# Numbering background convolution work 240 places later in a list-scheduled hybrid decoder layer

## The chip, the cores and the metric

The kernel runs on one core of a Trainium2 chip. The time is the device time of one execution in microseconds (us); less is better. The core's engines each work off a queue of their own: TensorE (PE; its weight loads are listed apart as PEld), VectorE (DVE), ScalarE (ACT), GpSimd (POOL) and SyncE (SP, which here only issues DMAs). An engine starts its instructions in the order of its queue.

## The reference

One layer of a hybrid decoder over a prompt of 2048 tokens and 8 single decode tokens, in fp32, with a model width of 1024:

```python
z = rms_norm(x, norm_mix_g) @ w_in
q, k, v, cu = jnp.split(z, [Q_END, K_END, V_END], axis=-1)
q = rope(rms_norm(q.reshape(B, T, N_HEADS, HEAD_DIM), q_norm_g), pos)
...
attn_o = banded_swa(q, k, v, attn_sinks)
...
a, g = jnp.split(cu, 2, axis=-1)
glu = a * jax.nn.sigmoid(g)
conv_ext = jnp.concatenate([conv_hist.astype(glu.dtype), glu], axis=1)
conv_o = jax.nn.silu(layer_norm(causal_dwconv(conv_ext, conv_w, conv_b), conv_ln_g, conv_ln_b))
h = x + jnp.concatenate([attn_o, conv_o], axis=-1) @ w_out
```

Attention has 8 heads of 64 over 2 key heads, a window of 128 and a sink per head. The convolution branch has 512 channels: a gated linear unit, a causal depthwise convolution of 31 taps, a LayerNorm over the channels, and swish. After it come a gated ConvFFN (2816 columns) and a sigmoid-gated per-layer embedding, which the change does not touch.

## The kernel before, in words

Every product that must be exact to fp32 is split into a high and a low part: `hilo` (line 211) copies the source to a reduced format on ACT and subtracts it on DVE, and `mm3` (line 194) multiplies three times on PE (lines 195 to 197).

**The attention stretch** goes through the prompt in four quarters of 512 tokens. A quarter has 12 slots, written out by hand in `orders` (line 867). An "a" slot is `ag_unit` (line 838): 24 matmuls of 512 columns into a PSUM tile, then a sigmoid on ACT (line 854) or, in every second unit, a product on DVE (line 860) and a store of the gated rows to DRAM. A "q" slot is `qkv_unit` (line 819): 48 matmuls (lines 828 to 833) into the tiles `pq` and `pk`, and a generator `attn_block` (line 588) that is taken forward by one stage in each of the next slots. In its stages the block normalizes and rotates q and k (DVE lines 532 to 578, POOL lines 221, 222, 539 and 576), transposes them on PE (lines 596 and 599) and copies them out split (line 213), multiplies scores (line 621), adds the mask and takes the minimum on DVE (line 627, one instruction per head, followed by a read of its accumulator), takes exponentials on ACT (line 631), reciprocals on DVE (line 636) and scales on ACT (line 639), transposes the probabilities (line 648) and multiplies by v (lines 659 to 662, tile `O`). Between quarters, `norm_x` (line 261) normalizes the next 512 rows and `xn_k` (line 308) transposes them (line 313). The first output-projection units follow in `w_out_unit` (line 776).

All transposes and small products of the kernel, those of the LayerNorm too, use the PSUM tag "T" (`ttile`, line 66), of which there are two buffers. The tiles of one tag get their buffers in program order: on PE the writers of T tiles stand in the order in which the program makes the tiles. The wide products of the stretch use the tag "mm", with four buffers.

**The background work** is the convolution. `conv_piece` (line 388) is a generator for one quarter: for each of four groups of 128 channels it loads 542 gated columns (line 397 or 399), multiplies once (line 408) and then adds 30 taps into the same tile, one `scalar_tensor_tensor` of 128x512 each (line 411), and at the end it runs `layer_norm` (line 427): three adds, a mean by a matmul on PE (`lnm`, line 435), a copy on ACT, subtractions, squares, a sum over channels on PE (`lnv`, line 455), a power on POOL, a transpose that spreads it (`lnb`, line 463), products, swish on ACT and a store from ACT's DMA queue (line 473). `bg(2500)` (line 510) is called after each slot and takes some five taps from the list. Two pieces are on the list in the attention stretch; the other two quarters are convolved in the feed-forward stretch.

**What sets the order.** The program runs once and numbers every instruction with a counter, `tc.cur_priority`. When it has ended, the framework's list scheduler goes through a modelled execution: whenever an engine is free in it, that engine gets, of the instructions whose inputs and buffers are ready, the one with the lowest number. The order so found is the order of each engine's queue on the chip. `bg` keeps the counter in `p0` and puts it back at its end, so the taps of a slot and the foreground of the next slot share the same numbers. Where a tap and foreground instructions are ready together, the lower number goes first; where only a tap is ready, it goes, however high its number. `later` (line 415) adds to the counter for a few instructions; the LayerNorm's PE instructions have 60 more that way.

Of the kernel before, what the change touches and what calls it, by code (L numbers as in the profile page):

```python
# [33 lines left out]
def hybrid_layer_kernel(ctx: ExitStack, tc: tile.TileContext, I, O):  # L34
# [472 lines left out]
    bg_list = []  # L507
    step_ns = [0]

    def bg(ns):  # L510
        p0 = tc.cur_priority
        while bg_list and ns > 0:
            try:
                c = next(bg_list[0])
            except StopIteration:
                bg_list.pop(0)
                continue
            if c == -1:
                break
            ns -= step_ns[0] if c is None else c  # L520
        tc.cur_priority = p0
# [197 lines left out]
    def new_R(nm, where, dt=F32R):  # L719

        return [RP[w].tile([128, 2, RW], dt, tag=f"R{w}", bufs=(16, 12)[w - 1], name=nm) for w in where]
# [157 lines left out]
    for q in range(4):  # L879
        ia = iq = 0  # L880
        L = len(orders[q])
        for si, ch in enumerate(orders[q]):
# [9 lines left out]
            else:  # L892
# [4 lines left out]
                live.append(ent)  # L897
            run_live()
            bg(2500)
            if q < 3:  # L900
                if si == (4, 2, 2)[q]:
# [31 lines left out]
    while live:  # L933
        w_out_unit(0, Rm0, mo, C0, acc)
        mo += 1
        run_live()
        bg(2500)
        slot += 1
# [122 lines left out]
        return range(n * (m - first) // c, n * (m - first + 1) // c) if m >= first else []  # L1061

    step_ns[0] = 1300
    Rm1 = new_R("mixA1", [1] * 8)
    for m in range(mo, KD):
        w_out_unit(0, Rm0, m, C0, acc)
        if m == 4:
            while bg_list:
                bg(1e9)
        elif m < 4:  # L1070
            bg(4000)
        fill_mix(Rm1, 0, 512, 512, ks=spread(m, mo))
        if m > 4:
            dec_step()
# [484 lines left out]
```

## Time and profile before

| | before |
|---|---|
| median of 3 runs (lowest to highest) | 2437.38 us (2435.72 to 2438.55) |
| the profiled execution | 2442.29 us |
| its span, first to last instruction | 2440.5 us |
| mean granted clock of TensorE | 0.987 |

The profile is of one execution. Its groups give, for each line and engine, the number of instructions, their busy time and the mean of one; its windows give the busy time of each engine in a stretch of the span, the clock that the throttle granted to PE as a share of full speed, the DMA engines' share and GB/s. A window's rows name, in this order, the stretch, its length, and then PE, PEld, DVE, ACT and POOL with their counts. The waits name an engine's instruction, what released it, the total, the number of times and the longest. The attention stretch takes about the first 500 us of the span, and its 240 taps (line 411) are 184.7 us of DVE's time between 50 and 500 us:

```profile
L411 DVE SCALAR_TENSOR_TENSOR co<-gi,cvec,co 128x512 f32<-128x512 f32 x240 | 184.7, 787 | 2.4
```

### The profile page before, as it was taken

How to read it: one execution, taken by the hardware profiler on the slowest of the kernel's cores; microseconds unless marked ns; L12 is line 12 of the kernel's file. 1: busy time of each engine (PE TensorE's matmuls, PEld its weight loads, DVE VectorE, ACT ScalarE, POOL GpSimd, SP SyncE). 2: the span in 40 equal slices, each digit the busy share in tenths (PEclk: the TensorE clock that was granted, in tenths of full speed). 3: DMA queues.
4: the chain of work that ended last, by engine and by line, in shares of the span. 5: the costliest groups of instructions: out<-in, count | busy, mean ns of one | idle time of the engine just before them, and what ended most of it. 6: DMA issues, size and time to landing. Idle time of an engine off the chain costs nothing.

```text
span 2440.5 us, 36702 instructions
## 1 busy us (share of the span) xinstructions
PE 2349.3 (96%) x13709; PEld 2035.6 (83%) x13709; DVE 1734.4 (71%) x2932; ACT 1188.4 (49%) x2186; POOL 290.1 (12%) x358
## 2 busy tenths in 40 slices
PE   7899999999899999999999998999999999999999
PEld 6777778877677777778778797999999999988889
DVE  4889879856799999779944469666666654465553
ACT  4566666665444444464333345444444543344443
POOL 3312232200011121110001002111111000000000
PEclk9999999999899999999999999999999999999999
DMA  8434332267322222355556661222222665666663
GB/s 293 168 113 138 136 96 73 81 213 228 113 87 83 83 86 84 91 168 189 191 166 190 201 187 57 79 78 78 77 82 79 207 213 180 200 215 201 201 188 114
DMA packets 357076, 348.19 MB, mean 143 GB/s; under 512 B 24414, under 2 KB 277784, under 8 KB 352770
## 3 DMA queue, kind: packets, MB, share of 16 engines
q1 hardware_dynamic: 336610, 333.25, 43.4%
q10 hardware_dynamic: 20288, 12.60, 1.8%
q8 instruction: 107, 1.75, 0.3%
q14 instruction: 71, 0.58, 0.1%
HBM read 271.61 MB, written 75.78 MB: 142 GB/s over the span
## 4 chain that ended last, share of the span: by engine, by line
PE 66%; DVE 17%; DMA 8%; ACT 4%; issue 3%; POOL 2%; SPq 0%; ACTq 0%; DVEq 0%
DVE co L411 5%; PE X L195 5%; PE X L196 5%; PE X L197 5%; PE fo L197 5%; PE fo L196 5%; PE fo L195 5%; DVE whl L213 3%; PE Z L195 2%; PE Z L196 2%; PE Z L197 2%; PE pg L195 2%; PE pg L196 2%; PE pg L197 2%; PE wo L195 2%
## 5 line engine op out<-in xcount | busy, mean ns | idle before, releaser
L213 DVE TENSOR_TENSOR whl<-raw,whl 128x1024 fp32r<-128x1024 f32 (+1 forms) x314 | 361.3, 1151 | 240.7 <-ACT whl L212 240.1
L212 ACT CAST whl<-raw 128x1024 fp32r<-128x1024 f32 (+1 forms) x314 | 310.0, 987 | 257.7 <-PE fo L197 135.8
L411 DVE SCALAR_TENSOR_TENSOR co<-gi,cvec,co 128x512 f32<-128x512 f32 x480 | 367.0, 788 | 2.9
L197 PE MATMUL fo<-act,whl 128*128 128x512 f32 (+2 forms) x880 | 308.5, 351 | 2.2 <-DVE whl L213 2.1
L195 PE MATMUL fo<-act,whl 128*128 128x512 f32 (+2 forms) x880 | 308.2, 350 | 1.9 <-DVE hs L1305 1.9
L196 PE MATMUL fo<-act,whl 128*128 128x512 f32 (+2 forms) x880 | 309.0, 351 | 0.0
L197 PEld LDWEIGHTS fo<-act,whl 128*128 128x128 f32 x880 | 165.4, 188 | 19.5 <-DVE whl L213 3.3
L195 PE MATMUL X<-T,whl 128*128 128x512 f32 (+2 forms) x528 | 173.3, 330 | 8.2 <-ACT whl L212 2.5
L195 PEld LDWEIGHTS fo<-act,whl 128*128 128x128 f32 x880 | 165.4, 188 | 17.6 <-DVE hs L1305 2.3
L196 PEld LDWEIGHTS fo<-act,whl 128*128 128x128 f32 x880 | 165.6, 188 | 15.9 <-issue 0.5
L196 PE MATMUL X<-T,whl 128*128 128x512 f32 (+2 forms) x528 | 172.3, 327 | 2.6 <-DVE T L1131 2.6
L197 PE MATMUL X<-T,whl 128*128 128x512 f32 (+2 forms) x528 | 170.8, 324 | 0.6 <-DVE whl L213 0.6
L1228 POOL TENSOR_TENSOR snB<-snB 128x256 f32<-128x256 f32 (+1 forms) x66 | 87.1, 1320 | 549.4 <-ACT snB L1219 549.4
L1181 ACT ACTIVATE ft<-ft 128x512 f32<-128x512 f32 (+2 forms) x110 | 60.2, 548 | 170.3 <-DVE ft L1176 129.8
L195 PEld LDWEIGHTS X<-T,whl 128*128 128x128 f32 x528 | 100.8, 192 | 24.5 <-ACT snA L1192 6.7
L195 PE MATMUL ag<-r,whl 128*128 128x512 f32 (+2 forms) x320 | 116.5, 366 | 0.0
L196 PE MATMUL ag<-r,whl 128*128 128x512 f32 (+2 forms) x320 | 115.0, 360 | 0.0
L197 PE MATMUL ag<-r,whl 128*128 128x512 f32 (+2 forms) x320 | 113.6, 355 | 0.0
L1173 ACT ACTIVATE ft<-ext,fvec 128x512 f32<-128x512 f32 (+2 forms) x110 | 80.0, 728 | 64.6 <-DVE ext L1195 32.7
L196 PEld LDWEIGHTS X<-T,whl 128*128 128x128 f32 x528 | 101.2, 192 | 11.2 <-DVE T L1131 4.0
L197 PEld LDWEIGHTS X<-T,whl 128*128 128x128 f32 x528 | 101.2, 192 | 9.1 <-DVE whl L213 1.1
L212 ACT CAST act<-act 128x512 fp32r<-128x512 f32 (+2 forms) x110 | 56.4, 535 | 73.9 <-DMA act<-actd 72.9
(382 smaller groups left out, 6400.8 us busy)
## 6 DMA issues: line engine op xcount, KB each, us to landing
raw<-in_w_ffn_out SPq DMA_DIRECT2D x110, 512.0 KB
raw<-in_w_ffn_in SPq DMA_DIRECT2D x88, 512.0 KB
whl<-agd SPq DMA_DIRECT2D x24, 1024.0 KB
hs<-h SPq DMA_DIRECT2D x80, 256.0 KB
raw<-in_w_out SPq DMA_DIRECT2D x32, 512.0 KB
raw<-in_w_ple_gate SPq DMA_DIRECT2D x32, 512.0 KB
actd<-ft SPq DMA_DIRECT2D x44, 256.0 KB
act<-actd SPq DMA_DIRECT2D x44, 256.0 KB
```

Of the source, the lines that this page charges most:

```text
L195: PE.matmul(ps, wh, xh, start=first, stop=False, skip_group_check=more)
L196: PE.matmul(ps, wh, xl, start=False, stop=False, skip_group_check=more)
L197: PE.matmul(ps, wl, xh, start=False, stop=last, skip_group_check=more)
L212: AC.copy(hi, src)
L213: DV.tensor_tensor(lo, src, hi.bitcast(F32), op=ALU.subtract)
L411: DV.scalar_tensor_tensor(co[c], t[:, i:i + QT], cvec[:, c, i:i + 1], co[c], op0=ALU.mult, op1=ALU.add)
L1173: AC.activation(t[:, :n], ext[:, 2 + o:2 + o + n], func=AF.Identity, scale=w2, bias=bi)
L1181: AC.activation(t[:, :n], t[:, :n], func=AF.Gelu)
L1228: GP.tensor_tensor(s3, s3, s5, op=ALU.add)
```

## The change

`bg` raises the counter by 240 before it takes its steps. The foreground of the next slots keeps its numbers, since `bg` puts the counter back. Where the attention stretch ends (before the rest of the first half's output projection), the list's value is set to 0, so the feed-forward stretch and the last steps of the second piece with its LayerNorm are numbered as before.

```diff
@@ -507,8 +507,11 @@
     bg_list = []
     step_ns = [0]
 
+    bg_late = [240]
+
     def bg(ns):
         p0 = tc.cur_priority
+        tc.cur_priority = p0 + bg_late[0]
         while bg_list and ns > 0:
             try:
                 c = next(bg_list[0])
@@ -1061,6 +1064,7 @@
         return range(n * (m - first) // c, n * (m - first + 1) // c) if m >= first else []
 
     step_ns[0] = 1300
+    bg_late[0] = 0
     Rm1 = new_R("mixA1", [1] * 8)
     for m in range(mo, KD):
         w_out_unit(0, Rm0, m, C0, acc)
```

No instruction is added or removed, and no tile is resized.

## The prediction

> **What bounds the kernel now.** I read the page first, then the windows of the attention stretch, then the waits of TensorE (PE) there, then VectorE (DVE) and ScalarE (ACT) instruction by instruction around each long wait. The page:
>
> ```profile
> span 2440.5 us, 36702 instructions
> PE 2349.3 (96%) x13709; PEld 2035.6 (83%) x13709; DVE 1734.4 (71%) x2932; ACT 1188.4 (49%) x2186; POOL 290.1 (12%) x358
> ```
>
> PE is busy for 2349.3 of 2440.5 us, so whatever can be won by order alone lies in the other 91.2 us and in time that PE spends at a lower clock. The change renumbers background work in the first 560 us or so; there the windows say
>
> ```profile
> 50.00:165.00 115.00, 102.66 (x544) 81.85 (x542) 100.98 (x191) 64.35 (x145) 36.16 (x39) 0.91 0.47 162
> 165.00:280.00 115.00, 111.44 (x630) 89.08 (x630) 109.28 (x224) 75.41 (x174) 22.26 (x30) 1.00 0.44 145
> 280.00:356.00 76.00, 66.22 (x346) 52.50 (x344) 55.97 (x117) 50.60 (x103) 22.95 (x20) 0.93 0.34 109
> 356.00:500.00 144.00, 141.67 (x988) 118.33 (x988) 127.76 (x300) 97.31 (x248) 34.49 (x44) 0.99 0.29 86
> ```
>
> (length, then busy time of PE, weight load, DVE, ACT and POOL, then the granted clock). Two stretches lose time: 50 to 165, where PE idles 12.3 us while DVE is busy for 101 of 115, and 280 to 356, where PE idles 9.8 us while DVE is not full. Their clock is low as well, 0.91 and 0.93. In 165 to 280 DVE is fuller than anywhere (109.28 of 115) and PE idles only 3.6 us at a clock of 1.00. So a full DVE by itself does not stop PE; what matters is whether the one DVE result that PE needs next stands behind others in DVE's queue.
>
> The longest waits of PE, and what follows three of them:
>
> ```profile
> PE O L659 <- DVE qT L213: 6.1, 1, 6.1
> PE xT L313 <- DVE qT L213: 3.7, 1, 3.7
> PE pk L830 <- DVE sig L860: 3.6, 1, 3.6
> PE PTp L648 <- ACT P L639: 3.4, 3, 2.7
> ```
> ```profile
> 63.88:67.45 3.57, 0.00 (x0) 0.00 (x1) 3.54 (x6) 0.13 (x1) 0.00 (x0) 1.00 0.80 335
> 97.49:100.16 2.67, 0.00 (x2) 0.00 (x1) 2.67 (x8) 2.09 (x7) 0.58 (x2) 0.86 0.18 30
> 124.45:128.18 3.73, 0.00 (x1) 0.00 (x0) 3.20 (x9) 3.71 (x12) 1.10 (x2) 0.81 0.14 35
> 68.72:72.13 3.41, 3.41 (x12) 2.82 (x11) 1.58 (x4) 0.00 (x0) 3.17 (x3) 0.50 0.92 203
> 99.44:106.27 6.83, 6.11 (x19) 4.87 (x20) 5.71 (x12) 4.38 (x11) 3.62 (x3) 0.50 0.60 192
> 126.75:136.99 10.24, 8.81 (x35) 7.01 (x36) 9.05 (x16) 3.19 (x9) 4.98 (x5) 0.50 0.00 0
> 300.82:307.65 6.83, 6.00 (x21) 4.41 (x20) 3.14 (x6) 3.16 (x7) 2.21 (x2) 0.50 0.30 89
> 352.02:358.85 6.83, 5.67 (x24) 3.99 (x24) 4.36 (x9) 5.11 (x11) 2.89 (x4) 0.50 0.15 37
> ```
>
> The first three rows are PE's idle gaps at 64, 97 and 124 us, each with DVE at work. The other five are stretches at a granted clock of 0.50, and each begins in, or within 1.3 us after, one of PE's five longest gaps, the shortest 2.67 us: a gap costs its own length and half of the slow stretch behind it. The three early gaps cost 3.57 + 2.67 + 3.73 = 9.97 us, and 3.41, 6.83 and 10.24 at half clock another 10.24 us, together 20.2 us. That is the stake.
>
> [...]
>
> **The change part by part.** It adds, removes and resizes no instruction. 240 taps (two pieces, four channel groups of 30, beside 8 opening multiplies) and the LayerNorm of the first piece get numbers 240 higher. The scheduler hands each engine the ready instruction with the lowest number, so a tap changes place only against foreground work that is ready at the same moment and numbered less than 240 above it.
>
> *Where that bites.* Counting the program's instructions, the first 60 or so taps run up to 50 to 170 numbers ahead of the DVE work next to them. Later ones run ahead of their own numbers, as fillers: around 200 us they stand some 100 behind the foreground beside them, around 450 us some 700, and 240 more changes nothing there. The change therefore acts in 50 to 165 us. What it does can be seen in the trace of before, in two batches of the same score reductions (L627):
>
> ```profile
> 117.46:119.39 1.93, 1.93 (x8) 1.00 0.95 365
> 122.24:126.17 3.93, 2.18 (x8) 1.00 0.29 69
> ```
>
> and, in the second of these windows, the taps (L411) alone:
>
> ```profile
> 122.24:126.17 3.93, 2.24 (x3) 1.00 0.29 69
> ```
>
> The first batch (four reductions and their four accumulator reads) has numbers 706 to 709 and the next taps 713 and up: it runs without a hole in 1.93 us. The second has 787 to 790 and the taps 715 to 717: a tap stands between each two, and it takes 3.93. With 955 to 957 these taps fall behind, as in the first batch.
>
> *The gap at 124 us* ends when ACT and DVE have copied qT out of PSUM; ACT's copy stands behind exponentials that wait for these reductions. Three taps less ahead of them are 3.93 - 1.93 = 2.0 us: 3.73 becomes 1.7. In the window from 200 to 220 us PE has one wait of that size,
>
> ```profile
> PE qTp L596 <- DVE PT L213: 1.7, 1, 1.7
> ```
>
> and no slow stretch behind it (clock 1.00 in 165 to 280), so 10.24 / 2 = 5.1 us go too. Term: 2.0 to 7.1, taken 7.1.
>
> *The gap at 97 us* waits for the normalized P, released by a reciprocal that has taps ahead of it:
>
> ```profile
> 97.62 0.73 DVE L408 TENSOR_SCALAR co<-gi,cvec 128x512 f32<-128x512 f32 x1
> ...
> 98.73 0.74 DVE L411 SCALAR_TENSOR_TENSOR co<-gi,cvec,co 128x512 f32<-128x512 f32 x1
> 99.40 0.26 DVE L636 RECIPROCAL den<-den 128x4 f32<-128x4 f32 x2
> ```
>
> These two, 503 and 504, pass behind the reciprocals, 547 and 612: the steps from start to start are 0.66, so 1.3 us less (a third tap, 500, fills a hole ahead of 499, which waits for its inputs, and may stay). Term: 1.3 us, and 3.4 us of slow clock, since the 1.4 us left are under every gap that was followed by one; at most the whole gap, 2.67 + 3.4 = 6.1; taken 4.7.
>
> *The gap at 64 us* waits for a sigmoid product (L860) behind a burst that found nothing else ready:
>
> ```profile
> 54.85 10.14 DVE L411 SCALAR_TENSOR_TENSOR co<-gi,cvec,co 128x512 f32<-128x512 f32 x9
> ```
>
> Fillers stay fillers, only the one tap next to the product passes it: 0.66 us of 3.57, clock unchanged. Term 0.7 (0 to 0.7).
>
> *The displaced taps* must run somewhere. All taps, and the first adds of the two LayerNorms, stand in these rows (count, ns, first and last start in us):
>
> ```profile
> L411 DVE SCALAR_TENSOR_TENSOR co<-gi,cvec,co x240: 714/744/2367, 54.9 to 469.8; 128x512 f32<-128x512 f32 x120
> L429 DVE TENSOR_TENSOR lns<-co x2: 655/670/685, 156.5 to 542.7; 128x512 f32<-128x512 f32 x2
> ```
>
> Some 50 taps at 0.744 us are 37 us. DVE is idle for 14.0 us in 50 to 165, 5.7 in the next window, 20 in 280 to 356 and 16.2 in 356 to 500. The second piece has its last tap at 470 us and its LayerNorm adds from 543, so 73 us are to spare. They fit, at nothing if they stay fillers; without that cover it is DVE's own time, and each hole closed late delays a foreground result by one tap, 0.66. I charge 1.0 (0 to 4).
>
> *The first LayerNorm* is moved too: adds, squares and multiplies on DVE and ACT, nine small matmuls and transposes on PE, a power on POOL, four stores on ACT's DMA queue and the loads of the next piece on SP's queue. The stores are read only in the last quarter. Behind a store in ACT's queue stand copies of the attention, but it waits only for the swish just ahead of it; behind the loads in SP's queue stand weight loads, which wait for PE in any case. I charge nothing for either. Its PE work matters:
>
> ```profile
> 278.89 1.02 PE L435 MATMUL lnm<-lns,oinv 128*128 128x512 f32 x2
> ...
> 299.56 1.02 PE L455 MATMUL lnv<-ones,lnsq 128*128 128x1 f32 x8 [2.87 <-DVE lnsq L448]
> ...
> 303.22 0.47 PE L463 MATMUL lnb<-ident,lnr 128*128 128x128 f32 x1 [0.83 <-POOL lnr L222]
> 303.35 0.77 PE L659 MATMUL O<-PT,v 128*128 128x512 f32 x1
> ```
>
> With 240 more projection matmuls queued ahead of lnv, PE should not wait for it: a gain of up to 2.87 + 0.83 + 6.83 / 2 = 7.1. Against that stands the first rival below. I take +3.5, a loss, half way between a gain of 7.1 and a loss of 14 (the rival's price without its slow clock).
>
> Sum: -7.1 - 4.7 - 0.7 + 1.0 + 3.5 = -8.0 us. The profiled execution took 2442.29 us, 1.8 us around its span, and would take 2434.3; it lies 4.9 us above the median of the runs shown, 2437.38, so the forecast for that median is 2429.4 us. About 0.2%, 4.9 us, is what a measurement of this kernel can tell from no change.
>
> **The rivals.**
>
> *Turns for the transpose tiles (slower).* All T tiles share two PSUM buffers and, in program order and trace alike, get them in program order: lnb, numbered 2173, ran before O (303.35), numbered 2126. So while lnm, lnv and lnb wait, no later attention block can transpose. Between the first two and O that is what is seen: projections run, attention stands still, DVE falls to 56 of 76 us and PE then waits 6.1 us for qT. At 240 later lnm also waits for a q unit and two more a units:
>
> ```profile
> 86.39:95.22 8.83, 8.73 (x49) 7.33 (x49) 7.21 (x18) 8.66 (x20) 2.25 (x3) 1.00 0.60 190
> 282.91:288.68 5.77, 5.77 (x26) 4.43 (x24) 5.28 (x16) 3.79 (x10) 1.18 (x3) 1.00 0.18 42
> ```
>
> That is 8.8 + 2 x 5.8 = 20.4 us by which attention falls back against projections. PE is not idle meanwhile; it pays where the projections of that quarter run out, before the next quarter's transposes. If two thirds come back as gaps, 14 us, and one slow stretch (3.4) with them, the net with the early gain of 11.5 is 17 - 11.5 = +6: 2443 us; with the early gain halved, 17 - 5.7 = +11. It decides once the lag exceeds what is left of projections, some 30 us in that quarter less what attention needs beside them. For it: 280 to 356 already loses 10 us of PE. Against: 356 to 500 shows PE at 141.67 of 144, so a lag was made good once.
>
> *Fillers stay fillers (no change).* Taps pass foreground work only when both are ready in the modelled order; on the chip a tap takes up to 2.4 us (the row of L411), DVE runs late, and the gaps may come from that lateness. Then early terms shrink to 0.7 + 1.3 + 2.0 = 4.0, the LayerNorm gives back 3.5: 2437 us. For it: the nine-tap burst and the 109.28 of 115 us.
>
> *Longer bursts block POOL.* Taps gathered in bursts can hold off POOL:
>
> ```profile
> 337.65 8.03 DVE L411 SCALAR_TENSOR_TENSOR co<-gi,cvec,co 128x512 f32<-128x512 f32 x12
> 339.17 6.58 POOL L221 TENSOR_SCALAR xss<-xss 128x4 f32<-128x4 f32 x1 [3.90 <-ACT junk L267]
> ```
>
> A POOL instruction on four columns ended only with the burst, ACT waited for it, and PE's 6.1 us gap came of it. One more such gap with its slow stretch is 6.1 + 3.4 = 9.5: -8.0 + 9.5 = +1.5, 2439 us. [...]
>
> **How the numbers follow.** Forecast case 0.46, fillers 0.22, POOL 0.08, turns 0.24. The forecast's own range: low end with all early terms at their most, 7.1 + 6.1 + 0.7 = 13.9, and the LayerNorm's gain of 7.1, 21 us under: 2416; high end 2433. The range reaches to the turns' worse value, +11: 2416 to 2449. Faster by over 0.2%: 0.45 (the forecast but for a sliver); within: 0.29; slower: 0.26 (the turns, and a little of POOL).
>
> **What would show it.** Right: no tap between the reductions before 165 us; the gaps at 97 and 124 us under 1.8 us and no clock of 0.50 behind them; PE near 108 of 115 us in that window; lnv without a wait. Wrong: the three gaps unchanged; or lnm some 20 us later against its projections, DVE emptier in 280 to 356, and new PE gaps at transposes between 300 and 420 us.

## The result, and the profile after

The changed kernel is slower: 2453.93 us median of 4 runs (2451.64 to 2461.10) against 2437.97 us (2435.72 to 2441.62) for the kernel before on the same chip, a ratio of 1.0069 with a 95% interval from 1.0045 to 1.0093. A second comparison on another chip (after_again, below) gave 1.0055, from 1.0034 to 1.0076. So the change costs 13 to 17 us, where 8 us less was forecast. The profiled execution took 2451.64 us, its span 2449.6 us, at a mean granted clock of 0.986.

In the code, what stands behind `bg` has moved down by 3 lines; the score reduction on DVE is now L630, the transposes of q and k are L599 and L602, the reciprocal is L639. The lines ahead of `bg` keep their numbers. The page of the changed kernel:

```profile
span 2449.6 us, 36708 instructions
PE 2347.2 (96%) x13709; PEld 2033.2 (83%) x13709; DVE 1728.2 (71%) x2932; ACT 1191.7 (49%) x2187; POOL 286.6 (12%) x358
```

The work is the same, to the matmul. PE is idle for 102.4 us where it was idle for 91.2. The same four windows as before, and then two gaps of PE with the half-clock stretch behind each (length; busy time of PE, weight load, DVE, ACT and POOL; granted clock):

```profile
50.00:165.00 115.00, 97.00 (x525) 77.74 (x523) 85.37 (x173) 61.72 (x138) 31.68 (x34) 0.93 0.47 159
165.00:280.00 115.00, 110.75 (x630) 88.04 (x630) 106.86 (x225) 77.35 (x179) 26.08 (x34) 1.00 0.43 140
280.00:356.00 76.00, 68.61 (x371) 54.39 (x369) 62.27 (x121) 45.75 (x93) 14.27 (x18) 0.99 0.34 113
356.00:500.00 144.00, 133.54 (x907) 109.20 (x908) 129.11 (x298) 98.21 (x249) 36.60 (x44) 0.96 0.26 77
...
125.28:132.28 7.00, 0.00 (x1) 0.02 (x1) 7.00 (x18) 2.76 (x10) 0.12 (x1) 0.57 0.36 112
350.73:360.32 9.59, 0.00 (x1) 0.03 (x1) 9.48 (x15) 8.83 (x13) 0.03 (x1) 0.72 0.15 56
...
126.27:136.51 10.24, 4.22 (x22) 3.13 (x22) 9.77 (x23) 5.16 (x14) 1.94 (x3) 0.50 0.25 76
354.96:368.61 13.65, 6.77 (x28) 4.81 (x30) 11.70 (x21) 9.64 (x20) 2.92 (x4) 0.50 0.16 53
```

The first stretch, which the change was to help, has lost 5.7 us of PE's work (102.66 became 97.00), although DVE has 15.6 us less to do in it. The last of the four has lost another 8.1. Two gaps stand out, and in both DVE is at work from end to end: 7.00 us at 125 us, where there were 3.73, and 9.59 us at 351 us, where there were 6.08 at 347 us.

**The gap at 125 us.** VectorE's rows around it (start, length, engine, line and operation):

```profile
117.60 0.53 DVE L630 CUSTOM_DVE_ANT_0 P<-S,mask,sinkb 128x256 f32<-128x256 f32 x1
118.07 0.08 DVE L630 DVE_READ_ACCUMULATOR2_ANT mx<- 128x1 f32 x1
118.07 0.74 DVE L411 SCALAR_TENSOR_TENSOR co<-gi,cvec,co 128x512 f32<-128x512 f32 x1
118.73 0.53 DVE L630 CUSTOM_DVE_ANT_0 P<-S,mask,sinkb 128x256 f32<-128x256 f32 x1
```
```profile
124.44 0.53 DVE L408 TENSOR_SCALAR co<-gi,cvec 128x512 f32<-128x512 f32 x1
124.90 4.05 DVE L411 SCALAR_TENSOR_TENSOR co<-gi,cvec,co 128x512 f32<-128x512 f32 x6
128.88 0.53 DVE L630 CUSTOM_DVE_ANT_0 P<-S,mask,sinkb 128x256 f32<-128x256 f32 x1
...
130.28 0.53 DVE L630 CUSTOM_DVE_ANT_0 P<-S,mask,sinkb 128x256 f32<-128x256 f32 x1
...
131.49 0.65 DVE L213 TENSOR_TENSOR qT<-qTp,qT 128x512 fp32r<-128x512 f32 x1
```

The picture of before is turned round. The batch of reductions that had no tap in it (numbers 704 to 707; the prediction's 706 to 709 is a miscount) has one between each two; the batch that had taps in it (787 to 790) runs without a hole, but behind an opening multiply and six taps in a row. Counting the program's instructions, these six are the taps 647 and 648 and 740, 744 to 746. They carry smaller numbers than the reductions behind them. Five slots in this stretch give their taps numbers from 404, 500, 552, 644 and 713 on, so 240 numbers are about three slots: the taps of 404 and 500, put back by 240, come due beside the attention that follows 713, and since each tap waits for the one ahead of it in its chain, those held back come due together, in one pile. The exponentials and the copy of qT wait for the pile, and PE waits for qT.

**The gap at 351 us.** ScalarE's rows, then VectorE's:

```profile
345.77 1.28 ACT L472 ACT_TABLE_LOAD   x1
347.06 0.81 ACT L472 ACTIVATE co<-co,cvec 128x512 f32<-128x512 f32 x1
347.79 1.04 ACT L267 ACTIVATE junk<-x 128x1024 bf16<-128x1024 f32 x1
...
350.79 4.26 ACT L270 ACTIVATE x<-x,xrs 128x1024 f32<-128x1024 f32 x4 [1.87 <-POOL xrs L222]
354.96 1.50 ACT L472 ACTIVATE co<-co,cvec 128x512 f32<-128x512 f32 x2
...
356.87 1.07 ACT L212 CAST PT<-PTp 128x512 fp32r<-128x512 f32 x2 [0.40 <-ACT co L472]
```
```profile
345.19 8.63 DVE L411 SCALAR_TENSOR_TENSOR co<-gi,cvec,co 128x512 f32<-128x512 f32 x11
...
354.19 5.38 DVE L411 SCALAR_TENSOR_TENSOR co<-gi,cvec,co 128x512 f32<-128x512 f32 x8
359.50 1.28 DVE L213 TENSOR_TENSOR PT<-PTp,PT 128x512 fp32r<-128x512 f32 x2
```

The LayerNorm's swish (L472) has landed among the operations that normalize the next 512 rows of x (L267 and L270). All of them stand in ScalarE's queue ahead of the copies of the transposed probabilities out of PSUM (L212). Both T buffers hold those probabilities, so the next qTp cannot start. VectorE fills the hole with taps, 19 in two runs, and its half of the copy comes another 2.6 us after ScalarE's first.

**The LayerNorm on PE**, as it answers to the rows of before:

```profile
304.11 1.02 PE L435 MATMUL lnm<-lns,oinv 128*128 128x512 f32 x2
```
```profile
319.81 1.02 PE L455 MATMUL lnv<-ones,lnsq 128*128 128x1 f32 x8
322.47 0.32 PE L463 MATMUL lnb<-ident,lnr 128*128 128x128 f32 x1 [0.95 <-POOL lnr L222]
```

lnm is 25 us later than before, behind a q unit and two more a units, and lnv has no wait. Measured against the projections, lnm starts 21.6 us after the end of the ninth query projection, where before it started as that unit ended. The attention is held back with it: O, which stands behind lnb in PE's queue, starts at 322.5 us instead of 303.35.

### The profile page after: what moved, and what is told of

The parts are those of the page before. It is cut to its first block, busy times and chain, and to the rows that moved or that the text cites. A ratio compares the mean times of both kernels' runs of the same rounds, so it can differ in the third digit from the quotient of the medians.

```text
span 2449.6 us, 36708 instructions
## 1 busy us (share of the span) xinstructions
PE 2347.2 (96%) x13709; PEld 2033.2 (83%) x13709; DVE 1728.2 (71%) x2932; ACT 1191.7 (49%) x2187; POOL 286.6 (12%) x358
## 4 chain that ended last, share of the span: by engine, by line
PE 65%; DVE 12%; DMA 7%; ACT 3%; issue 2%; POOL 1%; SPq 0%; ACTq 0%; DVEq 0%; POOLq 0%
PE X L195 6%; PE X L196 6%; PE X L197 6%; PE fo L196 4%; PE fo L197 4%; PE fo L195 4%; DVE co L411 4%; PE Z L195 3%; PE Z L196 3%; PE Z L197 3%; PE pg L195 2%; PE pg L196 2%; DVE whl L213 2%; PE pg L197 2%; PE wo L195 2%
## 5 line engine op out<-in xcount | busy, mean ns | idle before, releaser
L212 ACT CAST whl<-raw 128x1024 fp32r<-128x1024 f32 (+1 forms) x314 | 310.1, 988 | 258.8 <-PE fo L197 134.3
L411 DVE SCALAR_TENSOR_TENSOR co<-gi,cvec,co 128x512 f32<-128x512 f32 x480 | 356.7, 770 | 2.4
L1232 POOL TENSOR_TENSOR snB<-snB 128x256 f32<-128x256 f32 (+1 forms) x66 | 92.1, 1396 | 548.9 <-ACT snB L1223 548.9
L196 PEld LDWEIGHTS X<-T,whl 128*128 128x128 f32 x528 | 100.9, 191 | 11.3 <-DVE T L1135 4.1
L212 ACT CAST act<-act 128x512 fp32r<-128x512 f32 (+2 forms) x110 | 56.5, 536 | 73.8 <-DMA act<-actd 73.5
```

Source lines behind the costliest of these rows:

```text
L196: PE.matmul(ps, wh, xl, start=False, stop=False, skip_group_check=more)
L212: AC.copy(hi, src)
L411: DV.scalar_tensor_tensor(co[c], t[:, i:i + QT], cvec[:, c, i:i + 1], co[c], op0=ALU.mult, op1=ALU.add)
L1232: GP.tensor_tensor(s3, s3, s5, op=ALU.add)
```

## The experiments

One number per kernel says little here, since a different order early in the stretch moves what comes later. So each kernel is given with its ratio to the kernel before on the same chip, and a table at the end of this section says where its trace gained and lost. All kernels compute the whole layer.

**Taps or LayerNorm.** The taps and the LayerNorm of a piece get numbers of their own:

```diff
+        n0, bg_late[0] = bg_late[0], ln_late[0]
+        tc.cur_priority += bg_late[0] - n0
         yield from layer_norm(conv_p, co, QT, 4, mixd[half], off)
+        tc.cur_priority += n0 - bg_late[0]
+        bg_late[0] = n0
```

taps_only (240 for the taps, 0 for the LayerNorm):

> The 240 numbers for the taps alone; the two LayerNorms of the attention stretch get none and stand behind 60 numbers on TensorE only, as before. Theory A (the moved LayerNorm costs the time: its matrix products and its turn of a transpose buffer 240 numbers later, its swish in the middle of the x normalization): 2438 us, within 3 of before, since the stretch up to 283 us came out 0.45 us late with all of the change in it. Theory B (postponed taps gather into bursts in VectorE's queue and the foreground's operations stand behind them): 2450 to 2454 us, all of the loss, and a TensorE gap of over 5 us near 350 us. Both see the gap near 125 us, 5 to 7 us with a burst of taps inside it, since the first taps lie as in the changed kernel.

ln_only (0 and 240):

> The 240 numbers for the LayerNorm alone; the taps stand among the foreground as before. Theory A: 2450 to 2456 us, lnm over 10 us later against the projections than before and a new gap of over 5 us behind it. Theory B: 2434 to 2440 us, lnv's wait of 2.87 us gone and nothing new. If A and B each hold a part, the two parts (this kernel's loss and that of the taps alone) add up to about 16 us.

And by time, with `bg_late[0] = (240, 0, 0, 0)[q]` at the head of each quarter, or (0, 240, 240, 240):

q0_only:

> The 240 numbers only while the first quarter of the positions is worked on (some 44 taps, all of channel tile 0 and a part of tile 1); from then on taps and LayerNorm stand as before. Theory A: 2436 to 2440 us (the early stretch is worth nothing net). Theory B: the gap near 125 us is there, 5 to 7 us, but the three of before are smaller; 2436 to 2441 us. A third theory C (any other order of the first taps shifts what comes later by as much): over 2446 us with the early taps alone.

q123_only:

> The other half: no number added in the first quarter, 240 from the second quarter on, for taps and LayerNorm. Theories A and B: 2450 to 2456 us, as the whole change, because what loses lies behind 283 us; the gaps at 97 and 124 us of the kernel before are as they were. Theory C: 2438 to 2444 us, as the late part alone then loses little.

Measured: taps_only 1.0004 (0.9993 to 1.0016), ln_only 1.0017 (1.0003 to 1.0032), q0_only 1.0046 (1.0029 to 1.0063), q123_only 1.0034 (1.0017 to 1.0052). Neither A nor B holds by itself. Theory C was right that q0_only would come out over 2446 us (2454.19), but q123_only loses too, which C denies. The taps and the LayerNorm apart lose 0.21% together, less than the 0.55 to 0.69% of the whole change; the two halves in time lose 0.80%, which agrees with the whole within the intervals. The gaps sort cleanly. The one of 6 to 7 us near 125 us is in the kernels whose first taps are late, taps_only and q0_only, and not in the other two; the one at 350 us, 9.59 and 9.60 us long, is in the kernels whose LayerNorm is late, ln_only and q123_only, and not in the first two. taps_only does without the 347 us gap of before as well (0.76 us there), which pays for its early loss. q0_only has a second loss of its own at 233 us, which comes up again below.

**Which part of the late LayerNorm.** The changed kernel again, and two kernels that move the swish alone:

```diff
-            AC.activation(co[c], co[c], func=AF.Silu, scale=cvec[:, c, CK + 1:CK + 2], bias=cvec[:, c, CK + 2:CK + 3])
-            AC.dma_start(dst[CC + c * 128:CC + (c + 1) * 128, off:off + n], co[c])
+            with later(-bg_late[0]):
+                AC.activation(co[c], co[c], func=AF.Silu, scale=cvec[:, c, CK + 1:CK + 2], bias=cvec[:, c, CK + 2:CK + 3])
+                AC.dma_start(dst[CC + c * 128:CC + (c + 1) * 128, off:off + n], co[c])
```

after_again:

> The changed kernel itself, beside the next three on one chip. Every theory: 10 to 17 us slower than the kernel before (ratio 1.004 to 1.007), with the two long TensorE gaps of its first profile again, near 125 us (7.0 us) and near 350 us (9.6 us). If one of the gaps is absent in this profile it is an accident of one execution and not the change.

swish_now (the diff above on the changed kernel):

> The whole change, but the last step of the LayerNorm, its four swish operations on ScalarE and the four stores behind them, gets no number added. Theory A1 (the late swish stands in ScalarE's queue among the operations that normalize x, and both ahead of the copies of the transposed scores): the 9.6 us gap near 350 us falls under 4 us with its 13.65 us of half clock, and the kernel is 5 to 10 us faster than the changed kernel, 2442 to 2450 us. Theory A2 (it is the late matrix products and their turns of the transpose buffers): the gap stays at 9 to 10 us and the time within 3 us of the changed kernel. Both: the 7.0 us gap near 125 us stays.

swish_late (the kernel before, with `later(240)` there):

> The kernel before, and only the swish step of the LayerNorm and its stores 240 numbers later. Theory A1: a gap of 5 to 10 us near 350 us with half clock behind it and 3 to 8 us slower than before, 2446 to 2451 us where before has 2443. Theory A2: within 3 us of before, lnm and lnv at the times of before.

taps_q123 (240 for the taps from the second quarter on, nothing for the LayerNorm):

> 240 numbers for the taps from the second quarter on; none for the taps of the first quarter and none for the LayerNorm: the part of the change that is left if the early bursts (7.0 us gap near 125 us) and the late LayerNorm are what costs. The kernel with all taps late came past 279 us 3.5 us later than before and past 369 us 1.3 us earlier; so with the early part as before: 3 to 6 us faster than before, 2437 to 2440 us where before has 2443, if the theory that the loss has these two sources is right; the same as before or slower if any other order costs by itself.

Measured: after_again 1.0055 (1.0034 to 1.0076), with both gaps again, 6.31 and 9.58 us. taps_q123 0.9977 (0.9962 to 0.9993), within what was expected. The other two came out the wrong way round: swish_now 1.0112 (1.0090 to 1.0134) and swish_late 0.9964 (0.9946 to 0.9983). With the swish out of the way the gap near 350 us grew to 14.95 us. The trace of swish_now says why; POOL, ACT, DVE, and the gap as a window:

```profile
361.66 6.32 POOL L221 TENSOR_SCALAR xss<-xss 128x4 f32<-128x4 f32 x1 [3.49 <-ACT junk L267]
```
```profile
369.11 4.26 ACT L270 ACTIVATE x<-x,xrs 128x1024 f32<-128x1024 f32 x4 [7.14 <-POOL xrs L222]
...
374.08 0.56 ACT L212 CAST qT<-qTp 128x512 fp32r<-128x512 f32 x1
```
```profile
359.89 8.03 DVE L411 SCALAR_TENSOR_TENSOR co<-gi,cvec,co 128x512 f32<-128x512 f32 x12
```
```profile
360.47:375.42 14.95, 0.00 (x1) 0.00 (x1) 8.20 (x14) 7.81 (x14) 7.33 (x2) 0.54 0.00 0
```

This is the prediction's third rival, which the trace of before shows too. The small step on POOL that finishes the x normalization falls beside a burst of twelve taps and takes 6.32 us; ScalarE's queue stands for 7.14 us, and the copy of qT, for which PE waits, stands behind it. In the changed kernel the same step takes 0.20:

```profile
349.01 0.20 POOL L221 TENSOR_SCALAR xss<-xss 128x4 f32<-128x4 f32 x1 [1.43 <-ACT junk L267]
```

It falls inside a burst as well, the eleven taps from 345.19 us shown above. The bursts differ: those eleven start 0.79 us apart (8.63 us in all), the twelve here and the twelve of before 0.66 us (8.03 us), so that the next starts before the last, 0.74 us long, has ended. In the order of the queue, the taps 0.66 us apart add in turn into the tiles of two channel groups, and those 0.79 us apart add into one tile, each starting 0.04 us after the one ahead, 0.75 us long, has ended. The opening multiplies (L408) of the sixth and the seventh group agree with this (150 taps, five groups, run ahead of the sixth in both kernels): in before they start at 312.53 and 313.78 us, both ahead of its twelve, and in the changed kernel at 334.98 and 353.74, on either side of its eleven. So the late LayerNorm removes this stall by accident and puts the swish in its place. What is bad at 350 us in both kernels is one thing: the x normalization, 4.26 us of scalings and the wait ahead of them, in ScalarE's queue in front of copies that free PSUM buffers.

**The x normalization taken apart.** The squares and the POOL step go two slots earlier in the second and third quarter; the four scalings become a function of their own, `scale_x`, and stay:

```diff
+                if si == (6, 4, 4)[q]:
+                    norm_x(q + 1)
                 if si == 6:
-                    norm_x(q + 1)
+                    scale_x(q + 1)
```

split_before (this alone on the kernel before):

> The kernel before, with the x normalization in two parts: the squares and the small rstd step on GpSimd two slots earlier (in the second and third quarter), the four scalings where they were. Theory M1 (in the kernel before, the 6.08 us gap at 347 us comes from GpSimd's rstd step, which took 6.57 us beside a burst of ten taps where it takes 0.20 alone, with ScalarE's queue idle behind it): the gap falls under 2 us, its half clock with it, and the kernel is 5 to 12 us faster than before, as much as the kernels in which the burst happened not to lie there. Rival (the burst only moves and stops another step): within 3 us of before, with a gap of over 4 us at another place.

split_after (this on the changed kernel):

> The changed kernel with the same split of the x normalization. Theory M2 (the 9.6 us gap near 350 us comes from ScalarE's order: squares, swish, the four scalings and swish again ahead of the copies of the transposed scores): the gap falls under 3 us and the kernel is 6 to 13 us faster than the changed kernel, 2 to 8 us slower than before or less. Rival (the late LayerNorm costs by its matrix products and buffers wherever the normalization is): the gap stays over 6 us, the time within 3 us of the changed kernel. The 6 to 7 us gap near 125 us stays by both.

no_early (the kernel before, with `bg(2500 if q else 0)` in the attention stretch):

> The kernel before, and no tap at all is issued in the first quarter; they all come later, so the total time is no measure, only the stretch up to 165 us. The reading of the prediction (taps between VectorE's foreground operations made the gaps near 97 and 124 us): both under 1.8 us, no half clock behind them, and the fifth projection of the queries past by 160.4 minus 6 to 12 us. Rival (other waits bound this stretch too): gaps of over 2 us stay in it without a tap, and it is under 5 us shorter.

taps_q123_swish (taps_q123 and swish_late together):

> Two parts of the change that came out faster by themselves: 240 for the taps from the second quarter on (0.9977 of before) and 240 for the LayerNorm's swish step alone (0.9964). If the parts act by themselves: 0.994, some 14 us faster than before. If both gained by the same thing, the GpSimd step at the x normalization not being held beside a burst (the long gap at 347 us gone in each): 0.996 to 0.998, no better than one alone.

split_before: 0.9972 (0.9960 to 0.9985). The POOL step takes 0.20 us, the 6.08 us gap is gone with its slow clock, and the gain is what M1 expected. The split moves the squares of x as well as the POOL step, so it does not tell which of the two the gap was due to:

```profile
340.00:356.00 16.00, 15.54 (x91) 11.97 (x90) 14.02 (x37) 10.42 (x24) 5.78 (x7) 1.00 0.27 85
```

split_after: 1.0055 (1.0035 to 1.0075), no better than the changed kernel, although the gap did fall as M2 says, from 9.59 to 2.15 us, and the 13.65 us of slow clock behind it to 3.41:

```profile
350.00:364.00 14.00, 11.65 (x58) 8.88 (x57) 13.96 (x26) 11.91 (x27) 3.17 (x2) 1.00 0.38 130
```

Between 160 and 573 us its trace loses 3.8 us against before, where the two traces of the changed kernel lose 7.8 and 4.6. So the gap's 16 us (9.59 and half of 13.65) were mostly not a net loss; where the stretch gives the rest back is not shown. Against split_before, on the same chip, the change costs 20.9 us (2454.64 for 2433.72). taps_q123_swish 0.9981 (0.9967 to 0.9995): no better than either part, so both gained by the same gap. That leaves the early stretch, which no_early (one run, 2441.79 us) shows almost without taps (four start before 111 us, the first at 94.47):

```profile
50.00:165.00 115.00, 106.40 (x601) 85.11 (x600) 82.21 (x176) 71.76 (x162) 34.14 (x41) 0.99 0.52 180
```

The gaps near 97 and 124 us are gone, the clock is 0.99, and the fifth query projection is through 7.3 us earlier. So the prediction was right that the taps made those gaps. The rival holds in part: gaps of 2.05 us at 69 us, 1.98 at 88 and 2.00 at 105 stay, the first two before any tap has run.

**Why 240 places made it worse.** Two readings were open: the taps come due some slots later, or taps fill holes of the modelled order at any distance.

taps_far (as taps_only with 2000 for 240):

> As the kernel with the taps alone late, but 2000 numbers for 240, so that no tap's number comes due before the foreground near it. Theory M3 (the 240 come due two to three slots later, as a pile: in the changed kernel six taps with the numbers 644 to 648 and 740 to 746 stand in one row ahead of the reductions 787 to 790): no burst ahead of the reductions near 125 us, the gap there under 2 us, and the fifth query projection past 5 to 10 us earlier than in the kernel with 240 (which had it at 164 us, before at 160). Time 5 to 10 us under before if the rest stays. Rival (taps fill holes of the modelled order at any distance): a gap of over 5 us stays near 125 us, the time within 3 us of before.

far_split (this, and the x normalization split):

> The same with the x normalization split as in split_before. If the early part (M3) and the x normalization (M1) act at different places and add: 2424 to 2430 us where before has 2441, 0.994 to 0.996. If the second is already gone with the taps' other order: as taps_far.

late_start (split, no number added, the taps from the second quarter on with `bg(3300 if q else 0)`):

> Split x normalization, no number added, but the taps begin in the program only in the second quarter and then with 3300 ns a slot for 2500: early taps are fillers as with 2000. M3: the gaps near 97 and 124 us under 2 us, 8 us earlier at 165 us; with the split 0.993 to 0.996 if the second piece of the convolution is ready in time, about 1.000 if its end comes too late for the output projection near 580 us, as with no early tap, where 14 us were lost there.

far_all (the change with 2000 for 240, LayerNorm and all):

> The change with 2000 for 240, for taps and LayerNorm. The rival of the prediction (the LayerNorm's transpose buffers keep their turn, so the attention's transposes stand behind it): lnm over 40 us later than before and new TensorE gaps of over 5 us at transposes between 290 and 420 us, 6 us or more slower than taps_far. If the buffers' turns do not matter: within 3 us of taps_far.

The early stretch is settled. In taps_far no tap stands in the batch 787 to 790 or right before it, and the place where the changed kernel had its 7 us gap has one of 0.55:

```profile
50.00:165.00 115.00, 106.49 (x582) 86.29 (x581) 76.90 (x172) 67.12 (x155) 34.20 (x39) 0.96 0.49 168
```
```profile
121.00:128.00 7.00, 5.98 (x40) 4.38 (x38) 6.91 (x22) 4.33 (x14) 5.00 (x5) 1.00 0.16 37
```

PE does 106.49 us of work there, where it did 97.00 with 240. The total is another matter: taps_far 1.0026 (1.0012 to 1.0040), with a gap of 8.24 us at the x normalization, where the POOL step takes only 0.69 us and the scalings in ScalarE's queue 4.27 (so a gap there needs no long POOL step); far_split 0.9980 (0.9968 to 0.9991), no better than split_before, so the early gain is given back later; late_start 1.0046 (1.0030 to 1.0062), a miss by both branches of what was expected: it is 8.8 us early at the eighth output projection and 3.2 late at the tenth, behind a wait of 5.00 us for the second piece. far_all: 1.0131 (1.0112 to 1.0149), lnm 40 us later than before, some 25 us slower than taps_far, with PE's waits from 290 to 420 us where the prediction's first rival put them:

```profile
PE qTp L599 <- DVE PT L213: 7.9, 3, 3.4
PE O L662 <- DVE qT L213: 6.1, 1, 6.1
PE lnv L455 <- DVE lnsq L448: 5.8, 1, 5.8
PE PTp L651 <- ACT P L642: 5.4, 2, 4.6
```

**Both places mended.**

after_mended (the changed kernel with `bg_late[0] = (2000, 240, 240, 240)[q]` and the split):

> The changed kernel with 2000 numbers for 240 in the first quarter only, and the x normalization split. If the two places are the whole loss: the gaps near 125 and 350 us both under 2.5 us and the kernel within 5 us of before, or faster (0.996 to 1.002), where the change with the split alone was 1.0055. If the displaced taps give the early gain back later, as in taps_far: past 279 us 6 us earlier than before, and no more than 3 us of it left at 530 us. If there is a third place of the late LayerNorm: above 1.003.

split_swish_late (split_before and swish_late together):

> The kernel before with the x normalization split (0.9972 alone) and the swish step late (0.9964 alone). One gain in both, the gap at 347 us: 0.996 to 0.998, no better than one of them. Two gains: 0.994 or under.

after_mended: 0.9986 (0.9973 to 1.0000), so the loss against before is gone; against split_before, which has the split and no number added (0.9972, on another chip), nothing is gained. It differs from split_after (1.0055) only in the number of the first quarter's taps. In split_after the pile makes a gap of 6.37 us at 130 us with 17.07 us at half clock, together 6.37 + 17.07 / 2 = 14.9 us, and at the fifth query projection the two traces are 13.2 us apart. So the pile accounts for that difference. The place of the pile in after_mended:

```profile
121.00:128.00 7.00, 5.97 (x40) 4.39 (x38) 6.91 (x22) 4.33 (x14) 5.00 (x5) 1.00 0.16 37
```

The gap near 350 us is 2.43 us, as expected. The early gain is not given back against before (7.6 us early at the ninth query projection, 7.8 at the eighth output projection), but split_before reaches the same 7.7 from 0.3.

split_swish_late: 0.9986 (0.9973 to 0.9999), one gain and not two. The versions that beat both kernels are swish_late, split_before and taps_q123, and their intervals overlap; split_before is the one that was made for a wait read in the trace.

**Where each trace gained and lost.** The end of a unit's last matmul on PE, in us later (+) or earlier than in the profiled execution of before: the fifth query projection (160.4 us there), the ninth (279.1) and the eighth output projection (572.7).

| kernel | 5th q | 9th q | 8th out | ratio |
|---|---|---|---|---|
| first taps 240 late: the change, first profile | +3.6 | +3.5 | +11.4 | 1.0069 |
| after_again | +6.7 | +8.0 | +11.3 | 1.0055 |
| taps_only | +3.7 | +3.5 | -3.3 | 1.0004 |
| q0_only | +6.5 | +14.8 | +15.3 | 1.0046 |
| swish_now | +7.9 | +7.7 | +22.9 | 1.0112 |
| split_after | +8.2 | +10.7 | +12.0 | 1.0055 |
| first taps as before: ln_only | -2.8 | -2.8 | +0.6 | 1.0017 |
| q123_only | -1.3 | +0.1 | +6.9 | 1.0034 |
| swish_late | -3.6 | -2.1 | -8.7 | 0.9964 |
| taps_q123 | -4.5 | -3.2 | -7.7 | 0.9977 |
| taps_q123_swish | -2.6 | -2.7 | -10.8 | 0.9981 |
| split_before | -3.2 | -0.3 | -7.7 | 0.9972 |
| split_swish_late | -3.6 | -2.3 | -10.7 | 0.9986 |
| first taps 2000 late: taps_far | -5.1 | -6.0 | +0.2 | 1.0026 |
| far_split | -7.0 | -6.7 | -8.7 | 0.9980 |
| far_all | -6.3 | -6.4 | +30.9 | 1.0131 |
| after_mended | -5.0 | -7.6 | -7.8 | 0.9986 |
| no first taps: late_start | -5.9 | -7.7 | -8.8 | 1.0046 |
| no_early | -7.3 | -7.9 | -15.9 | |

At the fifth query projection the six kernels with 240 stand at +6.1 on average, the eight with the taps as before (the profile of before, 0, among them) at -2.7, the six with far or no taps at -6.1. So the 240 cost 8.8 us there. The eight kernels of the second group have the same order in every engine's queue up to 166 us, so their spread at this mark, 0 to -4.5, is that of one order from run to run, and the profile of before, from which the prediction was read, is the latest of the eight. q0_only's further 8 us up to the ninth come where its first x normalization meets a burst: its POOL step takes 3.36 us at 225 us, and PE then waits for 4.71, with 6.83 us at half clock behind it.

## Why the prediction was wrong

*That taps among the reductions cost the early stretch 10 to 20 us* was right in kind. Without them (no_early, taps_far) the gaps near 97 and 124 us go, and the stretch is shorter, but by 3.4 us against the mean of the kernels with taps as before, not by 11.5. Other waits of about 2 us take their place (no_early). And part of the stake was chance: the 6.83 us of slow clock behind the gap at 97 us, counted with 3.4, is absent from six of the eight profiles with this order, and behind the gap at 124 us six of them have 6.83 us where the profile of before has 10.24.

*"With 955 to 957 these taps fall behind, as in the first batch"* is the step that failed. The three taps looked at did fall behind. The step did not ask which taps come due at that place instead: those of about three slots before, renumbered from 404 to 408 and 500 to 506 into 644 to 648 and 740 to 746. An offset moves the whole row of taps along, and the collision with it; the chain ahead had held some of them back, so they came as a pile of six and an opening multiply, 4.5 us, where there had been three single taps. The term of 7.1 us gain became a gap of 7.00 us for 3.73 with the same 10.24 us of slow clock, or of 17.07 (after_again). With 2000, where nothing comes due, the gap is 0.55 us: that is shown. The same count of numbers with which the prediction found that the change "acts in 50 to 165 us" would have shown 240 numbers as three slots. That statement did not hold either: taps_q123 moves only taps from the second quarter on, and it is 0.23% faster, without the gap at 347 us.

*The gap at 97 us* went, but 2.24 us at xT (113.6 us) and 3.54 at pk (85.5 us) are in its place, each with 3.41 us of slow clock near it. The one at pk has no tap near it. *The gap at 64 us* went whole, and not by the one tap that was counted: the first tap now starts at 89.68 us instead of 54.85, so the burst is gone from there. The 2.05 us gap at 68 us waits for a POOL step (qn) and is in no_early too. With the taps as before the gap at 64 us varies from 1.7 to 3.6 us, so a term of 0.7 cannot be told.

*The displaced taps* at 1.0 us were about right while they are fillers, but not free: far_split enters the second half of the stretch 6.7 us early and leaves it no better than split_before. This return is seen in the table; its mechanism is not shown. DVE's busy time from 356 to 500 us does not tell the kernels with late taps (124 to 137 us of 144) from those with the first taps as before (124 to 136).

*The first LayerNorm*, +3.5 as half way between -7.1 and +14. Between the fifth query projection and the eighth output projection the kernels with LayerNorm and late taps lose 7.8, 4.6 and 8.2 (q123_only), the late LayerNorm alone 3.4. So the size was in the range. The gain in it came as said, lnv's wait is gone. The loss came as the first rival's sign list said (lnm 25 us later, a new gap at a transpose near 350 us) but not by its mechanism alone. The LayerNorm's turn did hold the attention back (O 19 us later). The T buffers that qTp waits for at 351 us, however, are kept by probabilities whose copies stand behind swish and x normalization in ScalarE's queue. DVE did not get emptier in 280 to 356 us either, it got fuller (55.97 to 62.27). With the split the gap goes while lnm stays as late against the projections, 21.6 us after the ninth query projection in split_after and after_mended as in the changed kernel, and after_mended has no loss; with 2000 numbers (far_all) the late LayerNorm does cost 25 us, through gaps at T tiles and at lnv itself. The prediction missed this because it looked for what the late step waits for, not at which queue positions its swish would take.

*Longer bursts block POOL* was the right mechanism at the wrong place: it is what the kernel before pays at 347 us, where the step takes 6.57 us (split_before gets 0.28% for it), and what swish_now pays twice over, with 6.32. The changed kernel avoids it: its step takes 0.20 us, beside a burst of the kind with 0.79 us between starts.

What stays open: the two places do not have fixed prices. The pile costs 0.27% between taps_q123 and taps_only and 0.69% between after_mended and split_after; the mended gap at 350 us brings nothing between after_again and split_after (each pair ran on two chips, and each ratio is to the kernel before on its own). A lead or a lag at 160 us may decide how the next x normalization meets the next burst, and no run here separates that from the price itself.

## What to carry to other kernels

Background work that gets an offset in a priority order is not put behind the foreground, it is put on top of other foreground: count the offset in units of the loop, and see what stands there. An offset larger than anything it can meet removed the pile but brought no gain over no offset (far_split 0.9980, after_mended 0.9986, split_before 0.9972), and on the LayerNorm it cost 1% (far_all). A gap read in one profile should be looked for in a second one before it is counted on. Before moving a step, list the queue positions of all that it issues on every engine, and see what they stand in front of; a copy that frees a PSUM buffer behind a long stretch of ScalarE's queue (here 4.26 us of scalings and the wait ahead of them) is the place to look at. And where the foreground has a small step on GpSimd beside long VectorE bursts (here 6.57 us beside twelve taps), issue it early enough that nobody waits for it: that was worth as much here (split_before, 0.9972) as the best reorderings (swish_late 0.9964, taps_q123 0.9977).

## What the runs showed of the hardware

The eleven taps from 345.19 us in the changed kernel, which add into one tile, start 0.79 us apart and last 0.75 us each; the twelve from 337.65 us in before, which add in turn into two, start 0.66 us apart and last 0.74. The small POOL step on four columns takes 6.57 and 6.32 us beside the twelve taps of before and of swish_now, and it ends 0.07 and 0.06 us after the last of them (345.75 and 345.68 us; 367.98 and 367.92). In q0_only and swish_late it takes 3.36 and 3.78 us. Beside the eleven of the changed kernel it takes 0.20 us, as it does there at 76.16 us, where no tap has run yet. What makes the difference between the two kinds of burst is not shown.

In before ScalarE stands idle for 7.40 us ahead of the scalings of x, and the copy of qT, which stands behind them in its queue, starts at 351.84 us, though the transposes that it reads had ended at 337.56.

Gaps of PE much shorter than those that the prediction counted, the shortest of them 2.67 us, are followed in some traces by a granted clock of 0.50. In late_start and in swish_late:

```profile
350.58:351.96 1.38, 0.00 (x0) 0.00 (x0) 0.74 (x2) 1.38 (x5) 0.00 (x0) 1.00 0.00 0
353.04:356.45 3.41, 3.41 (x13) 2.65 (x14) 1.68 (x4) 0.44 (x1) 2.89 (x4) 0.50 0.00 0
```
```profile
157.35:158.77 1.42, 0.00 (x1) 0.00 (x1) 0.51 (x1) 0.46 (x2) 0.93 (x1) 1.00 0.30 118
159.91:163.32 3.41, 3.41 (x17) 2.36 (x14) 1.90 (x4) 1.76 (x3) 2.37 (x3) 0.50 0.22 54
```

In ln_only the same gap, 1.42 us at 158.16, has a clock of 1.00 behind it, so the length alone does not decide. In before a gap of 1.25 us, at 1356.57, has 3.41 us at 0.50 behind it as well, from 1358.96; so the 1.4 us that the prediction left of the gap at 97 us were not too short for a slow stretch. In before and in the changed kernel every stretch at 0.50, but for the last of each trace (1.55 and 4.54 us), lasts 3.41, 6.83, 10.24 or 13.65 us, which are multiples of 3.41; 17.07, five times that, is seen in after_again, split_after, swish_now and q0_only.
